# A hybrid RWKV/gMLP block with a mixture of experts: the second norm's shift and the last weight splits on VectorE, the list of further blocks behind the operand transposes, small recurrence matmuls in turn over array parts

## The chip, the cores and the metric

The kernel runs on one core of one Trainium2 chip. The metric is the device time of one execution in microseconds. The numbers below are from repeated timings of the kernel before and from one profiled execution of it. Engines are named as in the profile: PE is TensorE (PEld its weight loads), DVE is VectorE, ACT is ScalarE, POOL is GpSimd, and SP is SyncE, whose queue starts most of the large transfers.

## The reference

One decoder block over a sequence of 1024 tokens of width 1024, all in float32. A first norm with a shift and scale computed from the vector c, one projection for two mixers (causal gMLP on half the width, RWKV-7 recurrence on the other half), one output projection, a second norm with its own shift and scale, and a mixture of 32 experts in 4 groups, two experts to a token. Cut to what the change touches:

```python
def _modulate(h, shift, scale):
    return h * (1 + scale[:, None, :]) + shift[:, None, :]

def reference(x, c, ...):
    mod = c @ ada_w[l] + ada_b[l]
    shift1, scale1, gate1, shift2, scale2, gate2 = jnp.split(mod, 6, axis=-1)
    h = _modulate(_rmsnorm(x, norm1_g[l]), shift1, scale1)
    z = h @ w_in[l]
    y_a = _gmlp_mixer(...)
    y_b = _rwkv7_mixer(...)
    y = jnp.concatenate([y_a, y_b], axis=-1) @ w_out[l]
    x = x + gate1[:, None, :] * y
    h = _modulate(_rmsnorm(x, norm2_g[l]), shift2, scale2)
    y = _hier_moe(h, router_group_w[l], ..., w_gate[l], w_up[l], w_down[l])
    x = x + gate2[:, None, :] * y
    return _rmsnorm(x, final_norm_g)
```

In `_rwkv7_mixer` a state of 64x64 for each of 8 heads runs through all tokens: it decays, is corrected along one vector and takes up the product of key and value; the output is state times r. In `_hier_moe` each token takes the best of 4 groups and in it the best two of 8 experts, and each expert computes `(silu(x @ w_gate) * (x @ w_up)) @ w_down` for its tokens.

## The kernel before

Work runs through four stages. **First** the vector c is turned into shifts, scales and gates, the first norm is taken and its result is split into a high and a low part, because the large products run as sums of products of such parts. Weights that come from HBM are split in the same way by `Stream.split`: ScalarE copies the high part (L282), another engine subtracts it from the raw weight (L284); `stream.eng` names that engine.

**Second** come the projection and the recurrence, for four quarters `q` of the sequence (`rwkv_unit`, L537 on; a quarter is a unit). A unit forms its products between keys and queries chunk by chunk (GR: `pch<-AR,kb`, L552, scaled into `GM`), solves a triangular system by blocks of 16 and 32 (L586 to L645: `pch<-s,GM`, `pch<-GM,s`), and carries the state over four chunks (L647 to L712: `akv` and the solve `pu` write two tiles, the state products `pch<-S,AR` and `py<-S,AR` use the old state S). Its matmuls use parts of the 128x128 array: 16, 32 or 64 rows and as many columns. The projection's large matmuls (`mm<-h,w`, `mm<-w,h`) are handed in between as filler.

**Third** is the output projection with the residual, in halves. Its last part (`outproj_b1`, L979 on) takes the second pair of `w_out` tiles through `Stream.split` with `stream.eng = [nc.gpsimd]` (`w<-wt,w`). Beside it `Rows.norm` normalises two row tiles at a time: VectorE scales (L1093), GpSimd adds the shift with a permuted read, so that a row lies in the order that the experts read (L1094), and the row is stored to `h2d` (L1095). Then follows the routing on VectorE (L1102 to L1185): logits L, group and expert choice by maxima and masks, the mask Mc of chosen experts, running counts, slots, and the table `tabT`. `expert_counts` sorts the experts by count; `tables` makes the index `idx` and weights `wrep` from `tabT`, `limits` the bounds `dg` and the counts `cnt`.

**Fourth** are the experts in sorted order (`positions`). Weight tiles of 2 MB go through a ring of nine; four places are loaded early, five use memory that is only free when the last row has been stored to `h2d`. A `Block` gathers the quarter rows of up to 128 tokens from `h2d` (L1527), transposes them to `xT` (L1534), multiplies them with gate and up weights (`mm<-wt,xT`), applies the activation and multiplies with the down weights (`pch<-wt,aT`). Position n + 1 is transposed and n + 2 gathered while n is computed. `lists` (L1600 to L1666) makes, in steps, the list of further blocks for experts with more tokens than their place holds; a last loop works on that list. At the end the rows are gathered back and the last norm is taken.

All of this is generated as one program, and the order on each engine is set by a scheduler that places instructions by priority as their operands become ready in its own account of time; each engine then runs its instructions strictly in that order. So a change of one instruction can move others that it doesn't name. `tc.issue_after(i)` tells the scheduler not to place what follows ahead of i.

## Time and profile before

| what | us |
|---|---|
| median of 3 runs | 1466.57 (1464.32 to 1468.75) |
| profiled execution | 1464.12 |
| its span in the trace | 1462.4 |
| PE / DVE / POOL / ACT busy | 1244.2 / 622.7 / 518.1 / 334.2 |
| DMA | 336.96 MB, mean 230 GB/s |

The span leaves 1.7 us of the profiled execution around it. Busy shares here are averages over the four stages, which have different limits; the rows below are therefore taken by stretch. In a timeline row the bracket names the idle time of the engine ahead of the instruction and what ended it. A busy vector instruction is not always a working one: an instruction that should be short and is long was held up after its start.

### The profile page before, as it was taken

The numbers are of one execution on the slowest core, as the hardware profiler recorded it, in microseconds if no ns is written. First come the engines' busy times: TensorE is split into PE (matmuls) and PEld (weight loads), VectorE is DVE, ScalarE is ACT, GpSimd is POOL, SyncE is SP. The second block draws the span as 40 slices with busy tenths as digits, with TensorE's granted clock in tenths as the row PEclk, the third lists the DMA queues.
The fourth block names the chain that finished last, engine by engine and source line by source line (L and its number), as shares of the span: only waits on it lengthen the run. The fifth ranks groups of instructions, "written<-read, shape, count | busy, mean of one in ns | idle before, by whom it ended". The sixth has DMA issues, their size and how long they took to land. (4 is left out here: it accounts for less than half of the span.)

```text
span 1462.4 us, 35772 instructions
## 1 busy us (share of the span) xinstructions
PE 1244.2 (85%) x15245; PEld 989.1 (68%) x15245; DVE 622.7 (43%) x1495; ACT 334.2 (23%) x619; POOL 518.1 (35%) x585
## 2 busy tenths in 40 slices
PE   4898888999997899989988449999999999989740
PEld 1576786768885788889975326686877788857520
DVE  2643853683246773772259761122111211112127
ACT  3634442233253543313232100000000000000002
POOL 4555421652354343542375652222111211110015
PEclk9989858997998879899987659999999999999875
DMA  8346325352225312340056388999999999999957
GB/s 309 91 141 235 104 62 159 89 173 74 58 69 174 94 38 66 102 163 31 23 212 252 144 342 290 398 416 410 417 415 413 354 418 417 417 416 382 375 192 282
DMA packets 125330, 336.96 MB, mean 230 GB/s; under 512 B 17016, under 2 KB 77364, under 8 KB 100592
## 3 DMA queue, kind: packets, MB, share of 16 engines
q1 hardware_dynamic: 88784, 273.44, 49.6%
q0 software_dynamic: 13584, 38.06, 7.0%
q10 hardware_dynamic: 22800, 23.12, 4.7%
q8 instruction: 122, 2.00, 0.6%
q14 instruction: 40, 0.33, 0.1%
HBM read 299.54 MB, written 38.44 MB: 231 GB/s over the span
## 5 line engine op out<-in xcount | busy, mean ns | idle before, releaser
L59 PE MATMUL mm<-wt,xT 128*32 128x256 f32 x5760 | 351.0, 385 | 46.4 <-issue 24.5
L59 PEld LDWEIGHTS mm<-wt,xT 128*32 128x32 f32 x5760 | 262.8, 111 | 123.9 <-issue 54.5
L59 PE MATMUL mm<-h,w 128*128 128x512 f32 (+2 forms) x864 | 225.9, 415 | 8.3 <-DVE h L354 3.2
L1527 POOL DMA_INDIRECT xg<-h2d,idx x90 | 92.3, 1026 | 354.2 <-DVE xT L1534 332.0
L59 PEld LDWEIGHTS mm<-h,w 128*128 128x128 f32 (+2 forms) x864 | 162.8, 194 | 55.0 <-DVE h L354 7.3
L59 PE MATMUL pch<-wt,aT 128*32 128x256 f32 x2880 | 184.5, 380 | 5.5 <-DVE yo L1576 1.7
L284 POOL TENSOR_TENSOR w<-wraw,w 128x512 fp32r<-128x512 f32 (+2 forms) x104 | 135.8, 1307 | 146.3 <-ACT w L282 145.3
L59 PEld LDWEIGHTS pch<-wt,aT 128*32 128x32 f32 x2880 | 130.6, 110 | 48.5 <-issue 20.0
L1554 DVE SCALAR_TENSOR_TENSOR sp<-mm,wrep,sg 128x128 f32<-128x128 f32 x90 | 31.9, 424 | 253.4 <-ACT sg L1551 253.4
L59 PE MATMUL mm<-w,h 128*128 128x256 f32 (+1 forms) x816 | 130.1, 313 | 8.3 <-DVE b L895 2.5
L1551 ACT ACTIVATE sg<-mm 128x256 f32<-128x256 f32 (+1 forms) x52 | 17.8, 355 | 488.6 <-PE mm L59 315.0
L59 PEld LDWEIGHTS mm<-w,h 128*128 128x128 f32 x816 | 114.0, 206 | 16.4 <-issue 2.9
L282 ACT ACTIVATE w<-wraw 128x512 fp32r<-128x512 f32 (+2 forms) x104 | 63.6, 614 | 95.4 <-PE mm L59 50.5
L59 PEld LDWEIGHTS pch<-s,GM 16*32 16x32 f32 (+2 forms) x1280 | 62.4, 134 | 18.2 <-DVE s L613 8.0
L59 PE MATMUL pch<-s,GM 16*32 16x16 f32 (+3 forms) x1280 | 66.8, 207 | 8.2 <-DVE s L613 7.0
L1534 DVE STREAM_TRANSPOSE xT<-xg 128x768 f32<-128x768 f32 (+2 forms) x33 | 29.4, 894 | 100.1 <-PE mm L59 100.1
L1576 DVE TENSOR_TENSOR yo<-pch,gate 128x512 f32<-128x512 f32 (+1 forms) x52 | 30.3, 610 | 76.5 <-PE pch L59 45.4
L1747 POOL DMA_INDIRECT wt<-ysd,rowi x16 | 16.6, 1036 | 98.4 <-DMA ysd<-yo 93.8
L59 PE MATMUL py<-aw,ccol 128*1 128x256 f32 x320 | 32.2, 476 | 16.4 <-DMA aw<-in_ada_w_dram 13.8
L556 DVE SCALAR_TENSOR_TENSOR GM<-pch,nsq,gmask 128x128 f32<-128x128 f32 x128 | 35.4, 339 | 2.5 <-PE pch L59 2.1
L59 PE MATMUL pch<-AR,kb 64*128 64x128 f32 x256 | 35.0, 327 | 0.9 <-DVE kb L473 0.9
L59 PEld LDWEIGHTS pch<-AR,kb 64*128 64x128 f32 x256 | 30.8, 225 | 6.0 <-issue 1.6
(418 smaller groups left out, 1645.8 us busy)
## 6 DMA issues: line engine op xcount, KB each, us to landing
wt<-in_moe_w_gate_dram SPq DMA_DIRECT2D x64, 1024.0 KB
wt<-in_moe_w_up_dram SPq DMA_DIRECT2D x64, 1024.0 KB
wt<-in_moe_w_down_dram SPq DMA_DIRECT2D x64, 1024.0 KB
aw<-in_ada_w_dram SPq DMA_DIRECT2D x48, 512.0 KB
wraw<-in_w_in_dram SPq DMA_DIRECT2D x80, 256.0 KB
ysd<-aw POOLq DMA_DIRECT2D x1, 8192.0 KB
ysd<-yo ACTq DMA_DIRECT2D x56, 96.0 KB
wraw<-in_w_out_dram SPq DMA_DIRECT2D x16, 256.0 KB
```

The source lines that it names most:

```text
L59: nc.tensor.matmul(*a_, **k_)
L282: nc.scalar.activation(hi, raw, AF.Copy)
L284: eng.tensor_tensor(lo, raw, hi.bitcast(F32), op=OP.subtract)
L556: nc.vector.scalar_tensor_tensor(GM[:, u, :], pg[:, c * P:(c + 1) * P], nsq[:, u:u + 1], gmask, op0=OP.mult, op1=OP.mult)
L1527: tc.keep_in_program_order(nc.gpsimd.indirect_dma_start(out=self.xg[:, 256 * g:256 * g + 256], out_offset=None, in_=h2q, in_offset=bass.In ...
L1534: nc.vector.transpose(self.xT[:, 0:self.ng].rearrange("p g k t -> p (g k t)"), self.xg[:, 0:256 * self.ng])
L1551: nc.scalar.activation(sg[:, g0:g0 + m, :], v[:, :, 0, :], AF.Silu)
L1554: nc.vector.scalar_tensor_tensor(self.sp[:, g0 + g, :].rearrange("p (b j) -> p j b", b=4), perm(v[:, g, 1, :]), self.wt(g0 + g), perm(sg[: ...
L1576: nc.vector.tensor_tensor(yo[:, g0:g0 + m, :], po[g0 // 2][:, 0:256 * m].rearrange("p (g f) -> p g f", g=m), gate2.unsqueeze(1).to_broadca ...
L1747: nc.gpsimd.indirect_dma_start(out=part(t, j), out_offset=None, in_=ysd, in_offset=bass.IndirectOffsetOnAxis(ap=rowi[:, t, j:j + 1], axis=0))
```

## The change

Five edits. The shift of the second norm is added by VectorE instead of GpSimd. The low parts of the last weights are subtracted by VectorE instead of GpSimd. The tensor `h2d` has 128 further rows, which an early store fills with zeros; the first three blocks' gathers carry no bounds check, the tiles that they fill are taken in another order and only their last quarter is cleared. `limits`, those clears and each step of `lists` are issued behind the latest operand transpose. In the recurrence the products over the two row halves, of the solve's two parts, of `akv` and `pu`, and of the two uses of the old state are written in turn, the last for even chunks only.

```diff
-    h2d = dram.tile([S, D], F32, name="h2d")
+    h2d = dram.tile([S + P, D], F32, name="h2d")
...
+            pgs = [c512() for h in range(2)]
+            for c in range(4):
+                for h in range(2):
+                    r = slice(64 * h, 64 * h + 64)
+                    mm_(pgs[h][:, c * P:(c + 1) * P], kb[r, c, :, :].rearrange("p a t -> p (a t)"),
+                                     AR[l][r, c, :, :].rearrange("p a t -> p (a t)"), start=True, stop=True)
             for h in range(2):
-                r = slice(64 * h, 64 * h + 64)
-                pg = c512()
...
+        pt = c512()
+        for u in range(32):
+            for b, r in enumerate((lo, hi)):
+                r16 = slice(r.start, r.start + 16)
+                mm_(pt[r, u * 16:(u + 1) * 16], GM[r16, u, 32 * b:32 * b + 32], AY[r16, u, 0:16], start=True, stop=True,
+                    skip_group_check=True)
         for b, r in enumerate((lo, hi)):
-            pt = c512()
...
+            if c % 2 == 0:
+                py = psy.tile([P, 512], F32, name="py")
+            t0 = (c % 2) * 64
...
+                    if t0 == 0:
+                        out_state(l)
...
+            pr, one = akv(c + 1) if c < 3 else (None, lambda *hd: None)
             for l, h, r, o in heads:
                 mm_(pu[64:128, o], GM[64:128, l * 8 + 2 * c + h, 0:64], R[64:128, o], start=True, stop=True)
+                one(l, h, r, o)
...
-        stream.eng = [nc.gpsimd]
+        stream.eng = [nc.vector]
...
-                nc.gpsimd.tensor_tensor(h2.rearrange("t (a b j) -> t a b j", a=4, b=KT), perm(tmp), perm(O["sh2"]), op=OP.add)
+                nc.vector.tensor_tensor(h2.rearrange("t (a b j) -> t a b j", a=4, b=KT), perm(tmp), perm(O["sh2"]), op=OP.add)
...
+        nc.gpsimd.dma_start(h2d[S:S + P, :], zt_)
...
-    for t_ in xgs:
-        nc.vector.memset(t_, 0.0)
...
+            skip = dict(bounds_check=4 * S - 1, oob_is_err=False) if Block.turn >= 3 else {}
+            self.xg = xgs[Block.turn % 3]
...
-    O["limits"]()
+    with tc.issue_after(Block.last.ins):
+        for t_ in xgs:
+            nc.vector.memset(t_[:, 768:1024], 0.0)
+        O["limits"]()
...
         if n > 1:
-            next(listing, None)
+            with tc.issue_after(Block.last.ins):
+                next(listing, None)
```

Lines of the changed kernel have other numbers: the scaling of the second norm is L1093 before and L1111 now, the shift addition L1094 and L1112, the mean's reduction L1102 and L1120, `limits` L1045 to L1052 and L1063 to L1070, the transposes L1534 and L1552, the clears L1509 and L1619.

VectorE at the last two row tiles, where `r` is the reciprocal root of the mean square, `b` the rows and L the logits. Before:

```order
L1102 TENSOR_REDUCE r_8000<-ss_7671 128x2 [waits Activation_49]
L145 TENSOR_SCALAR r_8000<-r_8000 128x2 [waits DVE_49]
L1085 TENSOR_TENSOR L<-mm,L 128x72 [waits PE_49]
L1104 TENSOR_TENSOR L<-L,r_8000 128x72 [waits DVE_49,Pool_49]
L1093 SCALAR_TENSOR_TENSOR b_8006<-b_7667,r_8000,b_6928 128x1024
L1105 TENSOR_TENSOR L<-L,RB 128x72 [waits DVE_49]
L1112 TENSOR_REDUCE gm<-L 128x2 [waits DVE_49]
L1113 TENSOR_TENSOR gq<-L,gm 128x8 [waits DVE_49]
L1146 TENSOR_TENSOR ex<-L,gm 128x2x4
```

Now:

```order
L1120 TENSOR_REDUCE r_7993<-ss_7664 128x2 [waits Activation_49]
L145 TENSOR_SCALAR r_7993<-r_7993 128x2 [waits DVE_49]
L1111 SCALAR_TENSOR_TENSOR b_7999<-b_7660,r_7993,b_6921 128x1024 [waits Pool_49]
L1195 TENSOR_TENSOR tabT<-tabT,tt 64x192 [waits PE_49]
L1112 TENSOR_TENSOR b_8000<-b_7999,b_6922 128x1024 [waits DMAHW5_49,DVE_49]
L1111 SCALAR_TENSOR_TENSOR b_8004<-b_7662,r_7993,b_6921 128x1024 [waits DVE_49]
L1103 TENSOR_TENSOR L<-mm,L 128x72 [waits PE_49]
L1112 TENSOR_TENSOR b_8005<-b_8004,b_6922 128x1024 [waits DMASW0_49,DVE_49]
L1122 TENSOR_TENSOR L<-L,r_7993 128x72 [waits DVE_49]
L1123 TENSOR_TENSOR L<-L,RB 128x72 [waits DVE_49]
L1130 TENSOR_REDUCE gm<-L 128x2 [waits DVE_49]
```

Both scalings and both shift additions now stand ahead of the routing's first maximum (`gm`); before, one scaling stood ahead of it, the other some twenty rows behind, and the additions were on GpSimd.

VectorE between the table `tabT` and the first expert, where `idx` is the index of the gathers, `sort` and `dg` belong to `limits`, `xg` is a gathered tile and `l_...` belong to `lists`. Before (the first transpose stands some forty rows of `lists` further on):

```order
L1046 TENSOR_REDUCE sort<-sort 64x1 [waits DVE_49]
L1047 TENSOR_SCALAR dg<-ident,sort 32x32 [waits DVE_49]
L1177 TENSOR_TENSOR tabT<-tabT,tt 64x192 [waits PE_49]
L1509 MEMSET xg_8172 128x1024 [waits DMASW7_49,DMASW6_49,DMAHW0_49,DMASW5_49,DMAHW1_49,DMASW1_49,Pool_49]
L1030 CAST eid<-tt 1x32 [waits PE_49]
L1509 MEMSET xg_8173 128x1024
L1509 MEMSET xg_8174 128x1024
L1630 MEMSET ov 1x99
L1639 MEMSET l_9098 1x32
L1038 TENSOR_SCALAR idx<-tt,acol 128x192 [waits PE_49]
L1052 COPY cnt<-tt 128x96 [waits PE_49]
L1609 TENSOR_TENSOR l_8740<-cnt 128x32 [waits DVE_49]
```

Now:

```order
L1195 TENSOR_TENSOR tabT<-tabT,tt 64x192 [waits PE_49]
L1048 CAST eid<-tt 1x32 [waits PE_49]
L1056 TENSOR_SCALAR idx<-tt,acol 128x192 [waits PE_49]
L1552 STREAM_TRANSPOSE xT<-xg_8165 128x768 [waits DMASW6_49,DMASW7_49,DMASW3_49,DMAHW0_49,DMASW2_49,DMASW0_49]
L1619 MEMSET xg_8165 128x256
L1619 MEMSET xg_8166 128x256
L1619 MEMSET xg_8167 128x256
L1063 TENSOR_TENSOR sort<-sort,posc 64x32 [waits DVE_49]
L1552 STREAM_TRANSPOSE xT<-xg_8166 128x768 [waits DMASW3_49,DMASW2_49,DMASW1_49]
L1064 TENSOR_REDUCE sort<-sort 64x1 [waits DVE_49]
L1065 TENSOR_SCALAR dg<-ident,sort 32x32 [waits DVE_49]
```

The transposes now follow the index at once, the clears stand behind the first transpose, and the rows of `limits` stand around the transpose of the second block. `dg` for the second bound and `cnt` follow within the next four rows.

TensorE at the same place, where `tt<-dg,ones` is the product of `limits` and `mm<-wt,xT` are the first expert's gate and up products. Before:

```order
L59 MATMUL tt<-sort,tabT 32x32 x23
L59 MATMUL py<-sort,tabT 32x32 x24
L59 MATMUL tt<-Mrun,ones 128x32 [waits DVE_49]
L59 MATMUL tt<-dg,ones 128x64
L59 MATMUL mm<-wt,xT 32x256 [waits DMASW5_49,DMASW2_49,DMASW6_49,DMASW1_49,DMASW7_49,DMASW0_49,DMAHW0_49,DVE_49,DMAHW1_49,PE_49,DMAHW7_49,Activation_49,Pool_49]
L59 MATMUL mm<-wt,xT 32x256 x47
```

Now:

```order
L59 MATMUL tt<-sort,tabT 32x32 x23
L59 MATMUL py<-sort,tabT 32x32 x24
L59 MATMUL tt<-Mrun,ones 128x32 [waits DVE_49]
L59 MATMUL mm<-wt,xT 32x256 [waits DMASW6_49,DMASW3_49,DMASW7_49,DMASW2_49,DMAHW0_49,DMASW1_49,DMAHW4_49,DMASW0_49,DMAHW5_49,DVE_49,DMAHW6_49,PE_49,DMAHW7_49,Activation_49,Pool_49]
L59 MATMUL mm<-wt,xT 32x256 x23
L59 MATMUL tt<-dg,ones 128x64 [waits DVE_49]
L59 MATMUL mm<-wt,xT 32x256 x24
```

The product of `limits` has moved from ahead of the first expert to behind its first 24 matmuls.

## Rows read from the trace of the kernel before

**Rows 1.** Table of windows, four stretches: start and end, length, busy us (and instructions) of each engine, the granted share of TensorE's full clock, the mean busy share of the DMA engines, GB/s.
```profile
60.00:745.00 685.00, 634.61 (x6001) 533.21 (x6001) 360.33 (x891) 256.72 (x449) 290.03 (x340) 0.88 0.33 101
...
757.60:819.90 62.30, 48.24 (x176) 35.99 (x177) 54.24 (x156) 16.28 (x32) 39.15 (x23) 0.72 0.65 257
...
850.40:867.00 16.60, 0.00 (x1) 0.03 (x1) 16.32 (x44) 0.00 (x0) 13.24 (x12) 0.50 1.02 414
...
940.00:1320.00 380.00, 365.64 (x6316) 291.21 (x6318) 72.47 (x147) 13.07 (x38) 68.01 (x68) 0.99 1.01 410
```

**Rows 2.** Timeline of all engines while the last two row tiles are normalised and routed: start us, length us, engine, line, operation, tile written and tiles read, shapes, count, and in brackets the idle time ahead of it with what ended it.
```profile
821.81 3.84 POOL L1094 TENSOR_TENSOR b<-b,b 128x1024 f32<-128x1024 f32 x1
...
822.39 0.16 DVE L1102 TENSOR_REDUCE r<-ss 128x2 f32<-128x4 f32 x1 [0.75 <-ACT b L1075]
...
822.58 3.11 DVE L145 TENSOR_SCALAR r<-r 128x2 f32<-128x2 f32 x1
...
825.77 0.71 POOL L146 TENSOR_TENSOR r<-r,nhalf 128x2 f32<-128x2 f32 x1
...
826.67 1.28 DVE L1093 SCALAR_TENSOR_TENSOR b<-b,r,b 128x1024 f32<-128x1024 f32 x1
...
828.12 0.16 DVE L1112 TENSOR_REDUCE gm<-L 128x2 f32<-128x8 f32 x1
...
828.32 3.52 DVE L1113 TENSOR_TENSOR gq<-L,gm 128x8 f32<-128x8 f32 x1
...
836.07 3.77 POOL L1094 TENSOR_TENSOR b<-b,b 128x1024 f32<-128x1024 f32 x1 [3.40 <-DVE aq L1114]
...
836.18 3.68 DVE L1152 SCALAR_TENSOR_TENSOR sg<-ex,sg 128x2 f32<-128x2 f32 x1
...
840.33 0.22 DVE L1135 TENSOR_TENSOR Mc<-Mall 128x64 f32<-128x64 f32 x1
```

**Rows 3.** The same timeline earlier, in the last output projection: one pair of GpSimd and VectorE.
```profile
765.04 3.88 POOL L1094 TENSOR_TENSOR b<-b,b 128x1024 f32<-128x1024 f32 x1 [1.93 <-DVE b L1093]
...
765.16 3.85 DVE L1161 TENSOR_TENSOR val<-Mall,tokf 128x64 f32<-128x64 f32 x1
```

**Rows 4.** Timeline from the table products to the first expert (the last row from the timeline of TensorE alone, which joins its matmuls).
```profile
847.05 0.81 PE L59 MATMUL py<-sort,tabT 32*32 32x32 f32 x43
...
848.76 0.91 DVE L1509 MEMSET xg<- 128x1024 f32 x1 [0.16 <-issue]
...
849.74 0.37 DVE L1038 TENSOR_SCALAR idx<-tt,acol 128x192 int32<-128x192 f32 x1
...
850.40 1.17 POOL L1527 DMA_INDIRECT xg<-h2d,idx  x1 [3.59 <-DVE cnt L1052]
...
854.49 1.00 POOL L1527 DMA_INDIRECT xg<-h2d,idx  x1 [0.30 <-issue]
...
865.72 1.82 DVE L1534 STREAM_TRANSPOSE xT<-xg 128x768 f32<-128x768 f32 x2
...
867.00 5.26 PE L59 MATMUL mm<-wt,xT 128*32 128x256 f32 x53 [17.96 <-issue]
```

**Rows 5.** DMA queues between 850.4 and 862 us: the queue that carries the gathers, its packets, MB, share of 16 engines.
```profile
q0 software_dynamic: 256, 0.44, 10.1%
```

**Rows 6.** Groups of instructions by line and shape over the whole execution, GpSimd and then VectorE: busy us, mean ns of one, idle us ahead of them and what ended it.
```profile
L1094 POOL TENSOR_TENSOR b<-b,b 128x1024 f32<-128x1024 f32 x8 | 31.0, 3874 | 10.4 <-DVE b L1093 4.1 <-DVE aq L1114 3.4 <-issue 1.6
...
L284 POOL TENSOR_TENSOR w<-wt,w 128x512 fp32r<-128x512 f32 x16 | 21.6, 1363 | 13.0 <-ACT w L282 12.9
...
L942 DVE TENSOR_TENSOR b<-b,b 128x512 f32<-128x512 f32 x4 | 2.6, 682 | 0.0
...
L1751 DVE TENSOR_TENSOR wt<-wt 128x1024 f32<-128x1024 f32 x8 | 9.8, 1223 | 15.6 <-DMA wt<-ysd,rowi 15.4
...
L1554 DVE SCALAR_TENSOR_TENSOR sp<-mm,wrep,sg 128x128 f32<-128x128 f32 x90 | 31.9, 424 | 253.4 <-ACT sg L1551 253.4
```

**Rows 7.** Timeline of SP's queue: the first issue of the ring's second part, and the first reissue into the ring.
```profile
843.87 0.80 SPq L1465 DMA_DIRECT2D wt<-in_moe_w_down_dram  x2
...
882.16 0.34 SPq L1458 DMA_DIRECT2D wt<-in_moe_w_gate_dram  x1
```

**Rows 8.** Table of windows, columns as in rows 1, one stretch of 5 us at the start of the experts.
```profile
875.00:880.00 5.00, 2.75 (x18) 0.76 (x21) 0.00 (x0) 0.00 (x0) 2.81 (x3) 0.80 0.27 67
```

**Rows 9.** Groups of VectorE between 757 and 840 us, columns as in rows 6.
```profile
L1161 DVE TENSOR_TENSOR val<-Mall,tokf 128x64 f32<-128x64 f32 x7 | 8.5, 1217 | 0.0
```

**Rows 10.** Groups of TensorE over the whole execution, columns as in rows 6. A float32 matmul leaves two records, so counts are twice the code's.
```profile
L59 PE MATMUL pch<-AR,kb 64*128 64x128 f32 x256 | 35.0, 327 | 0.9 <-DVE kb L473 0.9
...
L59 PE MATMUL pch<-s,GM 16*32 16x16 f32 x512 | 23.0, 197 | 7.0 <-DVE s L613 7.0
...
L59 PE MATMUL pch<-GM,s 32*16 32x16 f32 x512 | 13.6, 178 | 0.0
```

**Rows 11.** Timeline of TensorE: one set of GR products, one set of products over one row half, and the first and the last of a stretch of 22 rows with 32 records in all, in which two products over the two row halves take turns.
```profile
117.70 1.71 PE L59 MATMUL pch<-AR,kb 64*128 64x128 f32 x16 [0.93 <-DVE kb L473]
...
673.75 1.14 PE L59 MATMUL pch<-VU,GM 64*64 64x64 f32 x16
...
678.90 0.50 PE L59 MATMUL pch<-s,GM 64*64 64x64 f32 x5
...
679.99 0.45 PE L59 MATMUL pch<-VU,GM 64*64 64x64 f32 x5
```

More of the change, by code (lines that the diff above doesn't have):

```diff
@@ L626, in rwkv_unit @@
         nc.vector.tensor_tensor(AY[lo, :, 0:16], AY[lo, :, 0:16], pt[lo].rearrange("p (u c) -> p u c", c=16), op=OP.add)
+        pt = c512()
+        for u in range(32):
+            for b, r in enumerate((lo, hi)):
+                r16 = slice(r.start, r.start + 16)
+                mm_(pt[r16, u * 16:(u + 1) * 16], Y[r, u, :], GM[r, u, 32 * b + 16:32 * b + 32], start=True, stop=True,
+                    skip_group_check=True)
         for b, r in enumerate((lo, hi)):
[L628 removed]
             r16 = slice(r.start, r.start + 16)
[L630 to L631 removed]
             nc.scalar.activation(GM[r16, :, 32 * b + 16:32 * b + 32], pt[r16].rearrange("p (u c) -> p u c", c=16), AF.Copy)
@@ L650, in akv, with one @@
             pr = c512()
-            for l, h, r, o in heads:
+            def one(l, h, r, o):
                 mm_(pr[64:128, o], GM[0:64, l * 8 + 2 * c + h, 0:64], VU[0:64, c, o], start=(l + h == 0),
                                  stop=(c + q == 0), skip_group_check=True)
-            return pr
+            return pr, one
         halves = ((slice(0, 256), nc.vector), (slice(256, 512), nc.scalar))
@@ L666, in rwkv_unit @@
         X["buf"] = [ec.tile([P, 33, 32], F32, name=f"s{i}").rearrange("p a b -> p (a b)") for i in range(2)]
-        pr = akv(0)
+        pr, one = akv(0)
+        for hd in heads:
+            one(*hd)
         py = None
```

31 lines of the change are left out of this document (10 added, 21 removed).

## The prediction

> **What bounds the kernel now.** I read the table of windows first, because one share of busy time would average over stages with different limits [rows 1]. Three limits stand in it. From 60 to 745 us (recurrence, with the input projection as filler) TensorE is busy for 634.61 of 685 us: nothing else comes near, so time taken out of its queue there is time saved, as long as the filler is ready. From 940 to 1320 us the DMA engines are busy all the time at 410 GB/s: the experts' weights bound this stage, and it can only begin earlier, not run faster. Between them lie the last output projection (757.6 to 819.9 us) and the routing. In the first VectorE is busy for 54.24 of 62.30 us and TensorE for 48.24; from 850.4 to 867 us TensorE does nothing.
>
> Then I read the timeline of the routing [rows 2]. A vector instruction of 0.15 us lasts 3.1 to 3.7 us wherever GpSimd is in its 3.8 us addition of the second norm's shift: the reduced sum's scaling (L145) at 822.58, L1113 at 828.32, L1152 at 836.18. The earlier rows show the same pair at 765 us [rows 3]. So GpSimd's additions are not beside VectorE's work but in its way.
>
> Last I followed the start of the experts backwards [rows 4]: first gate/up matmul 867.00, its operand's transpose 865.72, first gather 850.40, index 849.74. The index waits behind three clears of 0.91 us, though its matmuls end at 847.86. The transposes come straight behind VectorE's list of further blocks, while 0.44 MB, more than the first block's three gathers of 128 rows of 1 KB (0.39 MB), have landed by 862 us [rows 5].
>
> **The routing and the start of the experts.** I keep 822.39, where the sums of squares of the last rows arrive, as the fixed point. Before, 17.94 us lie between it and Mc at 840.33. In the new order both scaled rows and both shift additions stand ahead of the routing chain, on VectorE. The reciprocal root is ready at 822.39 + 0.16 + 0.16 + 0.71 + 0.1 of gaps = 823.5 [rows 2]. Two scalings of 1.28, two additions of X, and about 1.0 of small ones follow. The chain from the group maximum (828.12) to Mc then takes 12.21 (to 840.33), less the two stalls of 3.37 and 3.54 and less a scaling of 1.28 that stood in it: 4.0 [rows 2].
>
> X is not in the trace: VectorE has no addition that permutes 1024 elements. The contiguous one takes 1.22 [rows 6]; the same permuted addition on GpSimd takes 3.87 [rows 6]. A vector instruction that scatters its output in steps takes 0.42 for 128 elements [rows 6], which by length would be 3.4. I take 2.2, the middle in ratio of 1.22 and 3.87, and keep both as bounds. The Trainium skill ("Advanced Engine Details and Errata", SBUF Cachelines) says that going to another 16-byte line at each access costs extra, and the permuted reads do that in steps of 32 bytes; it gives no price, so by it the sum only lies above that of 1.22.
>
> With 2.2: 823.5 + 2.56 + 4.4 + 1.0 + 4.0 = 835.5 at Mc, 4.8 earlier. Without the clears the index follows its matmuls at once (849.74 against 847.86, 1.9), and the gather no longer waits for the count behind it (0.2): 6.9 in all, first gather at 843.5. The last h2d rows are written some 8 us earlier, and with them the ring's next 10 MB of weights, which SP issues from 843.87 on [rows 7]: the gathers still travel under full queues, so I leave their 11.6 us (850.40 to 862), landing at 855.1. Now the transposes come next on VectorE, 0.91 each [rows 4]; first matmul at 856.3 against 867.00: 10.7 earlier.
>
> One wait is new. TensorE's queue has 24 gate/up matmuls, then tt<-dg,ones, which needs two vector results that stand behind the transpose of the second block. That block's gathers follow 4.1 us behind (854.49 against 850.40) [rows 4], so its transpose can begin at 859.2 and dg is there at about 861. The 24 matmuls are 48 records at 53 in 5.26 us [rows 4]: TensorE comes to the wait at 861.1. I take 1 us, with 3 as upper bound; the rest of block one and everything after is queued behind it. SP reissues weights at 882.16, 15.2 us behind the first matmul [rows 7], and the engines stand at 27% DMA share meanwhile [rows 8]: this moves with TensorE. From there on the stage is DMA bound, so what is won here reaches the end: **10 us** (4 with X of 3.87 and 3 of wait, 13 with X of 1.22 and none). The list of further blocks now runs between the experts, where VectorE is busy for 72 of 380 us [rows 1]; I cost it at nothing. If it did delay an operand's transpose, its steps of up to 1.2 us would show as TensorE waiting. The zero rows are one 0.5 MB store in the first stages, where the DMA share is 0.33 [rows 1]: nothing.
>
> **The last output projection.** 16 splits leave GpSimd (1.36 each) for VectorE, where a subtraction of this length takes 0.68 [rows 6]: 10.9 us, and four of the additions, 8.8 with X of 2.2. Against these 19.7 go 8.1 us of idle VectorE and the stalls. One line alone shows their size: seven L1161 take 8.5 us in all [rows 9], at 0.22 each for Mc of the same size [rows 2], 7.0 lost. Over all small instructions of this stretch I estimate some 20 us. So VectorE ends about where it was, while each split comes 0.7 sooner behind ScalarE. The stretch cannot go below TensorE's 48.24, a gain of 14; if no stall went it would be 12 longer. I take **5 us**.
>
> **The recurrence.** The GR products (pch<-AR,kb) fill 35.0 us of TensorE [rows 10]. With the two row halves in turn, into two tiles, they may overlap. The nearest row: products over one row half take 1.14 for 16, while the same in turn over both halves, as the scheduler already has it for two other products, take 32 in 1.54 (678.90 to 680.44) [rows 11], 48 ns instead of 71, a ratio of 0.68. For GR this gives 11 us; since its records are twice as long, I take 9, between 0 and 17. The first solve stage fills 23.0 us [rows 10], 45 ns a record; its sister with 32 rows has 27 ns (13.6 for 512). Reaching that gives 9; I take 6, between 0 and 9. The Trainium skill ("TensorEngine Tiling (Array Packing)", Gotcha 1: PSUM Pressure) says that row tiles cannot access one PSUM bank at the same time; this stage now writes both row groups into one bank, so by it these 6 are 0 and the sum is 6 less. The remaining solve stage already runs at 27 ns; the new order of the output-state products is hardly realised. Against this: evacuations that ran beside the second half of a stage now begin when both are done, about 1.2 us for each of four units, 5 in all. Net **10 us**, with -8 and +24 as bounds, since the scheduler shuffles the filler anew.
>
> **Sum.** 10 + 5 + 10 = 25 from the profiled execution's 1464.12 gives 1439; the runs' median is 2.45 above that execution, so 1442.
>
> **Rivals.**
> Alternation buys nothing: TensorE takes the two row groups one after the other, and later evacuations eat the rest. For it: GR's 107 ns a record (16 in 1.71 us [rows 11]) may be streaming alone. Against it: the row halves in turn of rows 11. Then the recurrence gives 0, and 15 remain: 1452.
> Alternation pays in full: GR 17 and solve 9, with the filler always ready, less 2: 24 in place of 10, 1428.
> The slower side: VectorE becomes the bound of the output projection. It runs in order, and the splits now stand behind the routing instructions, four scalings and four additions. If the additions take GpSimd's 3.87 there (15.5) and the stalls were not GpSimd's doing, 10.9 + 15.5 - 8.1 = 18 us are added, TensorE waits for each split, and the recurrence gives nothing; the start then gives only 4: 1466.6 + 18 - 4 = 1481. It decides from the point where the added vector time exceeds what the stalls give back by more than the other two gains, 4 to 20 us. Against it: the pairs of rows 2 and 3.
> The start does not come: the gathers land when the weights let them, near 865, whenever they were issued, and the recurrence's gains are taken by the filler's new order. Then only some 3 remain: 1463.
>
> **Chances.** Forecast 0.46, nothing from alternation 0.22, in full 0.13, start does not come 0.10, slower 0.09. About 0.3% (4.4 us) is what a measurement of this kernel can tell from no change. Of these cases the first three are faster (0.81), the fourth is the same (0.10), the last slower (0.09). The range takes in the first three cases, with 8 us below the lowest for bounds that add up, and ends at the fourth, where 2 in 10 are left out: 1420 to 1463; the forecast's own is 1434 to 1450.
>
> **What would show it.** Right: no vector instruction of small size above 0.5 us between 757 and 842; L1112 between 1.2 and 3.9 us; clears behind the transposes; first matmul about 10 us closer to Mc's row; the SP reissue moved alike; pch<-AR,kb clearly below 35.0 us and pch<-s,GM 16*32 below 23.0. Wrong: TensorE waiting for w<-wt of VectorE between the projection's matmuls; a wait for dg of several us; the recurrence ending at the same time as before with less busy time on TensorE.

## The result

The changed kernel takes 1416.84 us (1413.33 to 1419.01, 4 runs) against 1467.38 before (4 runs): a ratio of 0.9656, 95% interval 0.963 to 0.9682. The profiled execution took 1416.36 with a span of 1414.6. It is 50 us faster, where 25 were forecast, and lies below the stated range.

**Where the time came from.** Four marks that both programs have cut the span: the first split of `outproj_b1`, the last rows' mean reduction, the experts' first matmul, and the end. Table of windows between them, before, columns as in rows 1. The first row runs from the first matmul of the first solve stage to the first split, the fourth from the experts' first matmul to the ring's first reissue, the fifth from the start to the reduction:

```profile
188.03:757.58 569.55, 534.62 (x5489) 451.63 (x5489) 294.53 (x730) 200.58 (x358) 233.03 (x257) 0.87 0.31 94
757.58:822.39 64.81, 50.09 (x190) 37.42 (x190) 56.01 (x157) 18.14 (x38) 41.40 (x27) 0.73 0.65 254
822.39:867.00 44.61, 9.37 (x134) 7.22 (x133) 41.31 (x113) 1.00 (x3) 27.15 (x21) 0.51 0.66 261
867.00:882.16 15.16, 11.81 (x103) 4.99 (x107) 0.54 (x1) 0.00 (x0) 9.99 (x10) 0.75 0.57 208
0.00:822.39 822.39, 727.46 (x6475) 595.29 (x6475) 450.76 (x1144) 304.94 (x548) 369.12 (x447) 0.87 0.39 125
```

The same stretches of the changed kernel:

```profile
181.53:724.72 543.19, 509.76 (x5487) 426.75 (x5486) 299.07 (x728) 203.28 (x365) 228.71 (x261) 0.88 0.32 97
724.72:778.55 53.83, 42.41 (x196) 34.35 (x197) 51.17 (x180) 20.05 (x42) 5.16 (x6) 0.82 0.85 347
778.55:809.60 31.05, 12.45 (x149) 9.53 (x148) 16.90 (x63) 1.74 (x4) 10.63 (x14) 0.55 0.73 289
809.60:834.82 25.22, 14.14 (x107) 7.05 (x111) 2.58 (x10) 0.00 (x0) 13.66 (x14) 0.59 0.59 220
0.00:778.55 778.55, 689.93 (x6457) 561.85 (x6458) 449.38 (x1165) 303.93 (x546) 324.90 (x427) 0.89 0.41 133
```

Up to the first split 757.58 became 724.72, 32.9 us won (forecast 10). The recurrence's own last product (`py<-VU,GM`) ends at 723.0 before and at 687.2 now, so the mark stands for the recurrence. The output projection went from 64.81 to 53.83, 11.0 won (forecast 5). From the reduction to the first matmul 44.61 became 31.05, 13.6 won. And from there to the end 595.4 became 605.0: 9.6 were given back, all of them before the first reissue, since from the reissue on it takes 580.2 and 579.8. 32.9 + 11.0 + 13.6 - 9.6 = 47.9, against 47.8 of the spans.

The marks do not divide the work sharply: in some of the kernels below, work that here comes ahead of the last reduction comes behind it, so that one stretch is shorter by some 10 us and the next longer. Where this happens, I give the sum from the first split to Mc, which is 82.75 before and 66.54 here.

**The ring.** The experts' stage is bound by its transfers (rows 1), so it can also be read from SP's queue. Timeline of the changed kernel, answering to rows 7:

```profile
790.62 0.80 SPq L1484 DMA_DIRECT2D wt<-in_moe_w_down_dram  x2
...
834.82 0.35 SPq L1477 DMA_DIRECT2D wt<-in_moe_w_gate_dram  x1
```

The ring's second part is issued 53.3 us earlier than before (843.87), and from that issue to the end it takes 624.0 us in place of 618.5. Between that issue and the first reissue the DMA engines are busy for a share of 0.75 of 44.2 us, before for 0.81 of 38.3: they stand idle for 11.0 us in place of 7.3.

**The recurrence.** Groups of TensorE over the whole execution, answering to rows 10:

```profile
L59 PE MATMUL pch<-AR,kb 64*128 64x128 f32 x256 | 28.8, 328 | 4.5 <-DVE GM L558 3.6 <-DVE kb L473 0.9
...
L59 PE MATMUL pch<-s,GM 16*32 16x16 f32 x512 | 10.9, 186 | 1.8 <-DVE s L615 1.7 <-DVE s L616 0.2
...
L59 PE MATMUL pch<-GM,s 32*16 32x16 f32 x512 | 8.0, 176 | 1.1 <-issue 1.1
```

The first solve stage fell from 23.0 to 10.9 us, 21 ns a record; its sister from 13.6 to 8.0, 16 ns; GR from 35.0 to 28.8. That is 23.9 us less. TensorE's busy time up to the first split fell by 29.9 in all (677.4 to 647.5) and its idle time by 3.0 (80.2 to 77.2), which makes up the 32.9.

**The routing.** Timeline of the last two row tiles and of the index, answering to rows 2 and 4:

```profile
778.55 0.16 DVE L1120 TENSOR_REDUCE r<-ss 128x2 f32<-128x4 f32 x1 [0.73 <-ACT b L1093]
...
778.74 0.17 DVE L145 TENSOR_SCALAR r<-r 128x2 f32<-128x2 f32 x1
...
781.27 2.03 DVE L1112 TENSOR_TENSOR b<-b,b 128x1024 f32<-128x1024 f32 x1
...
784.68 1.98 DVE L1112 TENSOR_TENSOR b<-b,b 128x1024 f32<-128x1024 f32 x1
...
790.89 0.16 DVE L1170 SCALAR_TENSOR_TENSOR sg<-ex,sg 128x2 f32<-128x2 f32 x1
...
791.26 0.22 DVE L1153 TENSOR_TENSOR Mc<-Mall 128x64 f32<-128x64 f32 x1
...
798.33 0.42 DVE L1056 TENSOR_SCALAR idx<-tt,acol 128x192 int32<-128x192 f32 x1 [0.89 <-PE tt L59]
...
799.04 1.10 POOL L1545 DMA_INDIRECT xg<-h2d,idx  x1 [1.18 <-DVE idx L1056]
```

The scaling L145 and L1170 (L1152 before) are back at 0.16 and 0.17 us, from 3.11 and 3.68. The permuted addition takes 2.0 on VectorE. From the reduction to Mc it is 12.7, from Mc to the first gather 7.8, against 17.9 and 10.1. From Mc to the end it is 623.3, against 622.1: behind Mc nothing is won.

**The start of the experts.** Timeline of TensorE from its first expert matmul:

```profile
809.60 4.53 PE L59 MATMUL mm<-wt,xT 128*32 128x256 f32 x42 [10.20 <-issue]
...
814.76 0.38 PE L59 MATMUL mm<-wt,xT 128*32 128x256 f32 x1 [0.63 <-issue]
...
816.90 0.59 PE L59 MATMUL mm<-wt,xT 128*32 128x256 f32 x1 [1.76 <-issue]
...
825.37 0.58 PE L59 MATMUL mm<-wt,xT 128*32 128x256 f32 x1 [2.23 <-issue]
...
827.98 0.47 PE L59 MATMUL tt<-dg,ones 32*128 32x64 f32 x1
...
829.10 10.87 PE L59 MATMUL mm<-wt,xT 128*32 128x256 f32 x144
```

After 42 records the matmuls come one by one, 2.8 us apart, with "issue" as the reason: nothing that the trace shows is waited for. The two small products of `limits` stand in the middle of this and not behind a wait: their vector results were there at 814.2. Only at 829.1 does TensorE run again. GpSimd's timeline in the same time, the first and the last of its gathers:

```profile
799.04 1.10 POOL L1545 DMA_INDIRECT xg<-h2d,idx  x1 [1.18 <-DVE idx L1056]
...
823.61 1.00 POOL L1545 DMA_INDIRECT xg<-h2d,idx  x1 [0.30 <-issue]
```

Between them GpSimd issues gather after gather, and two scatters (L1207), with pauses of 0.3 us; two more scatters follow at 825.77 and 829.02. Before, there was the same: 53 records, then three to five in 1.4 us up to 878.44, while the gathers ran until 878.4. One row of TensorE's timeline before:

```profile
875.58 0.64 PE L59 MATMUL mm<-wt,xT 128*32 128x256 f32 x5 [0.78 <-issue]
```

I call this the slow stretch. Of the two queues that load instructions, q8 moves nothing and q14 one packet of 0.01 MB between 813 and 829.1 us in the changed kernel, so a late load on q8 does not explain it.

### The profile page after: what moved, and what is told of

It reads as the page before. It is cut to its first block, busy times and chain, and to the rows that moved or that the text cites. A ratio compares the mean times of both kernels' runs of the same rounds, so it can differ in the third digit from the quotient of the medians.

```text
span 1414.6 us, 35774 instructions
## 1 busy us (share of the span) xinstructions
PE 1211.0 (86%) x15245; PEld 960.1 (68%) x15245; DVE 612.7 (43%) x1519; ACT 334.1 (24%) x619; POOL 462.8 (33%) x562
## 5 line engine op out<-in xcount | busy, mean ns | idle before, releaser
L284 POOL TENSOR_TENSOR w<-wraw,w 128x512 fp32r<-128x512 f32 (+2 forms) x104 | 131.6, 1269 | 148.0 <-ACT w L282 147.7
L1569 ACT ACTIVATE sg<-mm 128x256 f32<-128x256 f32 (+1 forms) x52 | 17.9, 355 | 485.8 <-PE mm L59 286.4
L1552 DVE STREAM_TRANSPOSE xT<-xg 128x768 f32<-128x768 f32 (+2 forms) x33 | 29.6, 896 | 113.8 <-PE mm L59 102.1
L59 PE MATMUL pch<-s,GM 16*32 16x16 f32 (+3 forms) x1280 | 54.5, 202 | 5.9 <-DVE s L671 2.7
L59 PEld LDWEIGHTS pch<-s,GM 16*32 16x32 f32 (+2 forms) x1280 | 49.5, 126 | 13.8 <-issue 7.0
L1770 POOL DMA_INDIRECT wt<-ysd,rowi x16 | 17.1, 1068 | 99.2 <-DMA ysd<-yo 94.7
L59 PE MATMUL py<-aw,ccol 128*1 128x256 f32 x320 | 29.6, 453 | 12.1 <-DMA aw<-in_ada_w_dram 11.9
L59 PE MATMUL pch<-AR,kb 64*128 64x128 f32 x256 | 28.8, 328 | 4.5 <-DVE GM L558 3.6
L59 PEld LDWEIGHTS pch<-AR,kb 64*128 64x128 f32 x256 | 24.2, 224 | 10.9 <-DVE GM L558 4.5
```

Of the source, the lines that this page charges most:

```text
L59: nc.tensor.matmul(*a_, **k_)
L284: eng.tensor_tensor(lo, raw, hi.bitcast(F32), op=OP.subtract)
L1552: Block.last = nc.vector.transpose(self.xT[:, 0:self.ng].rearrange("p g k t -> p (g k t)"), self.xg[:, 0:256 * self.ng])
L1569: nc.scalar.activation(sg[:, g0:g0 + m, :], v[:, :, 0, :], AF.Silu)
L1770: nc.gpsimd.indirect_dma_start(out=part(t, j), out_offset=None, in_=ysd, in_offset=bass.IndirectOffsetOnAxis(ap=rowi[:, t, j:j + 1], axis=0))
```

## The experiments

Ratios are to the kernel before on the same chip. Markers are read from each kernel's profile as above. The last six kernels ran on a chip on which the kernel before takes 1454 us, 10 to 15 less than on the others.

### Parts alone

The two solve stages alone:

```diff
+        pt = c512()
+        for u in range(32):
+            for b, r in enumerate((lo, hi)):
...
+                mm_(pt[r, u * 16:(u + 1) * 16], ...)
```

> The kernel before with one part of the change: the two parts of the solve's first and last stage in turn. Theory A (the array's row groups really work at once, and TensorE's queue is what bounds the recurrence): pch<-s,GM 16*32 falls from 23.0 to about 11 us and pch<-GM,s 32*16 from 13.6 to about 8, and the time falls by about the 18 us of both, to about 1449. Theory B (the 33 us won ahead of the projection come from a new order of the filler, whatever part is changed): the two groups shorten, but the time falls by less than 8 or by more than 25 us, without relation to them. By the rule that row tiles cannot use one PSUM bank at once the first group would stay at 23; the trace of the changed kernel already speaks against that.

Measured 0.9982 (0.9954 to 1.0011): 3 us, and within its interval of nothing. Groups and window up to the last reduction:

```profile
L59 PE MATMUL pch<-s,GM 16*32 16x16 f32 x512 | 12.4, 193 | 5.6 <-DVE s L613 3.9 <-DVE s L614 1.7
...
L59 PE MATMUL pch<-GM,s 32*16 32x16 f32 x512 | 7.7, 177 | 0.6 <-issue 0.6
```

```profile
0.00:822.23 822.23, 709.25 (x6472) 575.17 (x6472) 455.89 (x1144) 303.67 (x547) 371.18 (x447) 0.88 0.39 125
```

The groups did what theory A says, and TensorE's busy time fell by 18.2 (727.46 to 709.25). The time did not: idle time rose from 94.9 to 113.0. The waits of TensorE in that kernel (engine, what for; total us, times, longest) show where:

```profile
PE py L59 <- DMA aw<-in_ada_w_dram: 12.9, 7, 2.5
...
PE mm L59 <- DVE b L900: 6.2, 1, 6.2
...
PE mm L59 <- ACT v L1257: 3.1, 2, 2.7
```

Before, the first was 6.9 and the second 2.5. The filler was not there when the shorter stage wanted it. So a smaller time in TensorE's queue is worth something only together with what follows.

GR alone (hunk as in the diff above).

> The kernel before with one part of the change: the GR products over the two row halves in turn, into two PSUM tiles. Theory A: pch<-AR,kb falls from 35.0 to about 29 us, and the time by 4 to 8 us, to about 1461. Theory B (order of the filler): a change of the time by more than 12 us either way.

0.9928 (0.9906 to 0.9951), 10.5 us. GR fell to 25.6, 9.4 less, the 9 of the forecast; busy time up to the reduction 716.51, 10.9 less, idle time 99.3. Here the busy time passed on, and more of it than the 4 to 8 of theory A.

The norm alone: L1094 and the splits on VectorE.

> The kernel before with the second norm's shift and the last splits on VectorE, nothing else. Theory A: nothing before the projection changes (first w<-wt copy within 5 us of 757.6); the stretch from there to the last rows' reduction shrinks from 64.8 by about 11 us, and the routing from that reduction to Mc from 17.9 to about 13; the start of the experts gets some 4 to 5 us of that; the end 10 to 16 us earlier, about 1454. Theory B: the recurrence also ends more than 8 us earlier, since the scheduler orders everything anew.

0.9875 (0.9809 to 0.9941), 18 us. The recurrence ended 9 us later (first split 766.63), which neither theory has. The projection shrank by 20, from 64.8 to 45.0, and the reduction to Mc stayed at 17.1; from the first split to Mc it is 62.08 in place of 82.75. Its two halves, on another chip:

```diff
-                nc.gpsimd.tensor_tensor(h2.rearrange(...), perm(tmp), perm(O["sh2"]), op=OP.add)
+                nc.vector.tensor_tensor(h2.rearrange(...), perm(tmp), perm(O["sh2"]), op=OP.add)
```

> The kernel before with the second norm's shift addition on VectorE, the splits still on GpSimd. Theory A (the additions of 3.9 us hold VectorE and, on GpSimd's queue, the splits behind them): most of the 20 us in the projection and the whole of the gain from the last reduction to Mc; about 1450. Theory B (the splits are the cause): under 6 us in all, about 1461.

```diff
-        stream.eng = [nc.gpsimd]
+        stream.eng = [nc.vector]
```

> The kernel before with the last splits on VectorE, the shift still on GpSimd. Theory A: the splits now wait in VectorE's order behind instructions that GpSimd's additions hold up, so little or nothing is won, 1461 to 1468. Theory B (the splits are the cause): most of the 20 us, about 1450.

Shift: 0.9902 (0.9879 to 0.9925), 14 us; projection 57.6, reduction to Mc 12.6. Splits: 0.996 (0.9939 to 0.998), 6 us; projection 53.2, reduction to Mc 18.9. Neither theory holds alone: of the stretch from the first split to Mc 12.6 go with the shift (70.12) and 10.7 with the splits (72.07), where both together gave 20.7. The kernel before was not profiled on this chip, so its stretches are from another. The splits alone lose part of it again: from Mc to the first matmul it is 30.6 in place of 26.7. One split in the second kernel took 3.26 us, the others 0.68; that an addition on GpSimd held it is argued.

The start of the experts alone (zero rows, no bounds check, clears, limits and list behind the transposes).

> The kernel before with the zero rows, the gathers without bounds check, and clears, limits and the list's steps behind the transposes, nothing else. The first matmul of the experts should come about 8 to 9 us earlier relative to Mc. Theory A (TensorE's first matmuls then crawl for want of instructions while the ring's transfers run, as the changed kernel shows, and the first reissue of a ring tile, 38.3 us behind the ring's start before, comes hardly earlier): the end is 0 to 4 us earlier, about 1465. Theory B (the start passes on to the end): 8 us earlier, about 1458.

0.9957 (0.9932 to 0.9981), 6 us. From Mc to the first matmul 19.4 in place of 26.7, and from there to the reissue 22.1 in place of 15.2: theory A for the stage. The 6 us come mostly from ahead of it: the reduction stood at 815.6 (822.39 before), though no instruction of the recurrence was changed; from Mc to the end it is 619.2 in place of 622.1. So a new order of the filler alone can do as much; the kernels below show still more.

### Parts taken back from the changed kernel

> The changed kernel with the solve's two stages put back to one part after the other. Alone this edit took 16.5 us out of TensorE's busy time and only 3 out of the kernel's, because TensorE waited 11 us more ahead of the projection. Theory A (the edit is worth its busy time wherever the filler is ready, as it is in the changed kernel): about 14 to 18 us slower than the changed kernel, 1431 to 1435. Theory B (parts add up as they do alone): 3 us slower, 1420.

0.9784 (0.9743 to 0.9825) against 0.9656: 18.8 us slower, just above the 14 to 18 of theory A. Groups, and the window up to the reduction:

```profile
L59 PE MATMUL pch<-s,GM 16*32 16x16 f32 x512 | 20.5, 190 | 1.6 <-DVE s L615 1.6
...
L59 PE MATMUL pch<-GM,s 32*16 32x16 f32 x512 | 14.1, 181 | 0.0
```

```profile
0.00:795.76 795.76, 711.01 (x6457) 582.57 (x6458) 447.72 (x1165) 305.19 (x547) 327.60 (x427) 0.87 0.40 131
```

The two groups take 15.7 more than in the changed kernel, and the first split comes 16.4 later (741.13). Up to the reduction busy time rises by 21.1 against the changed kernel's 689.93, the stretch by 17.2. In this company the edit's busy time passes on; alone it was worth 3.

> The changed kernel with the GR products put back to one row half after the other. Alone this edit took 9.4 us of TensorE's busy time and 10.5 of the kernel's; in the changed kernel pch<-AR,kb is only 6.2 below before, with 3.6 of new idle time ahead of it (waiting for the scaling into GM). Theory A (busy time and its waits): 3 to 7 us slower than the changed kernel, about 1422. Theory B (parts add up as alone): 10 slower, 1427. More than 12 or faster: the order of the filler decides.

0.9653 (0.9607 to 0.97): nothing lost, which neither theory has. pch<-AR,kb is 37.5, 8.7 more than in the changed kernel, but the reduction comes at 783.1, busy time 693.58, only 3.7 more: other groups became cheaper in that order.

> The changed kernel with the shift and the last splits back on GpSimd. Theory A (the 18 us that this edit is worth alone lie behind the recurrence and are independent of it): the stretch from the first split to the last reduction goes from 53.8 back to about 65, that from there to Mc from 12.7 to about 18; 12 to 18 us slower, about 1432. Theory B (with the recurrence shorter, another wait takes its place): under 8 us slower.

0.9735 (0.9688 to 0.9783): 11.6 us slower, a little under the 12 to 18 of theory A. Projection 66.2, reduction to Mc 18.3, both as it says; the recurrence unchanged (first split 725.2).

> The changed kernel with clears, limits, bounds checks and the list's steps as before. Theory A (of the 8 us by which the first matmul comes earlier, TensorE's crawl behind it gives nearly all back): Mc to first matmul goes from 18.3 to about 26.7, first matmul to the first reissue from 25.2 to about 15, time 0 to 3 us slower. Theory B (the 6 us that the edit is worth alone): about 1423, with the difference ahead of the projection and not in the start of the experts.

0.9633 (0.9581 to 0.9686): not slower. Mc to the first matmul went back to 26.0, first matmul to reissue to 16.3, so in the stage nothing was lost by taking the edit out: from Mc to the end it is 622.5, in the changed kernel 623.3. Ahead of it the order happened to be better (first split at 718.8, Mc at 783.4 in place of 791.3).

> The changed kernel with akv, pu and the two products with the old state written one after the other again. The scheduler had put akv and pu in turn already, and their groups are unchanged (21.3 against 21.0, 20.5 against 20.4, 18.5 against 18.0, 16.8 twice). Theory A: nothing is lost, within 5 us of the changed kernel by the filler's order. Theory B (this is where the rest of the recurrence's 33 us comes from): 6 to 12 us slower.

0.9719 (0.9688 to 0.9751): 9 us slower, the time of theory B. Window up to the first split:

```profile
0.00:737.79 737.79, 654.80 (x6285) 535.09 (x6285) 411.48 (x995) 288.61 (x515) 322.69 (x422) 0.89 0.38 119
```

The recurrence's end came 13.1 us later than in the changed kernel, with 7.3 more busy and 5.8 more idle time. Then the projection took 44.4 and the reduction to Mc 23.6, in place of 53.8 and 12.7: from the first split to Mc 67.92, 1.4 more. So the loss lies ahead of the first split. The edit's four groups take 21.1, 21.3, 19.0 and 17.5 us, 1.8 more than in the changed kernel (21.3, 20.5, 18.5 and 16.8). This run does not show whether the rest is the edit's or that of a new order of the filler: the kernel of the next section loses as much without a longer solve group.

### One bank or two

```diff
-        pt = c512()
+        pts = [c512() for _ in range(2)]
...
-                mm_(pt[r, u * 16:(u + 1) * 16], ...
+                mm_(pts[b][r, u * 16:(u + 1) * 16], ...
```

> The changed kernel with the two parts of each solve stage in PSUM tiles of their own instead of one. Theory A (row groups that write other partitions of one bank do not disturb each other): pch<-s,GM 16*32 stays at 21 ns a record (10.9 us) and pch<-GM,s 32*16 at 16 (8.0), time within 6 us of the changed kernel, by the filler's order alone. Theory B (the shared bank costs something): both groups shorten by over a fifth.

```profile
L59 PE MATMUL pch<-s,GM 16*32 16x16 f32 x512 | 10.4, 180 | 2.3 <-DVE s L615 1.2 <-DVE s L616 1.1
...
L59 PE MATMUL pch<-GM,s 32*16 32x16 f32 x512 | 8.2, 175 | 3.8 <-issue 3.8
```

The groups stay (10.4 and 8.2 against 10.9 and 8.0): with or without a shared bank the two row groups take the same time. The Trainium skill ("TensorEngine Tiling (Array Packing)", Gotcha 1: PSUM Pressure) says that row tiles cannot access one PSUM bank at the same time. I had read a cost into that, by which the first group would have stayed at 23 us; the trace shows none for these two row groups, which write different partitions of the bank. The time, 0.9726 (0.9694 to 0.9758), is 10 us above the changed kernel, where theory A allowed 6; the first split comes 17.0 later (741.7). Busy time is lower (684.76 up to the reduction) and idle time higher (102.7 against 88.6). The groups answer the question; that the filler was less ready, as in the solve alone, is argued.

### What TensorE's slow stretch hangs on

In all the kernels up to here the time from the first gather to the first reissue was 31 to 36 us, whatever the first matmul did. To see whether the gathers cause that, those from the third position on were held back until the first activation:

```diff
+        if n == 0:
+            nc.gpsimd.tensor_copy(idx2[:, 0, 0:1], positions[0].blocks[0].sg[:, 0, 0:1])
+            nc.gpsimd.tensor_copy(idx2, idx)
```

> The changed kernel, but from the third position on the gathers read a copy of the index that GpSimd makes behind ScalarE's first activation, so that only the first six gathers run while TensorE does its first products. In every trace so far TensorE's slow stretch (one to five records in 1.4 to 2.8 us, nothing waited for) ends 1 to 3 us behind GpSimd's unbroken row of gathers, whether the weights' transfers were then running or not. Theory A (the row of gathers starves TensorE of instructions): no slow stretch; first matmul to first reissue 15 us in place of 25; up to 10 us faster than the changed kernel, about 1407, less what comes back when the held gathers run. Theory B (the ring's 10 MB of weights starve it): the slow stretch stays until the transfers are done, reissue 36 to 44 us behind the ring's start, time within 3 us of the changed kernel.

> The same hold on the kernel without the edits at the start of the experts (clears, limits and list ahead of the transposes). There the slow stretch lay where the DMA engines were busy for only 0.2 to 0.5. Theory A: no slow stretch, first matmul to first reissue falls from 16.3 to about 11, up to 5 us faster than without the hold (1410.8). Theory B: unchanged.

0.9774 (0.9747 to 0.98) and 0.9788 (0.9762 to 0.9814), 17 and 23 us slower than the kernels without the hold. TensorE in the first, GpSimd's held row, and the window of 840 to 850 us:

```profile
812.17 5.35 PE L59 MATMUL mm<-wt,xT 128*32 128x256 f32 x48 [10.35 <-issue]
...
818.01 7.98 PE L59 MATMUL mm<-wt,xT 128*32 128x256 f32 x144
...
835.43 0.64 PE L59 MATMUL mm<-wt,xT 128*32 128x256 f32 x4 [0.80 <-issue]
...
846.75 1.72 PE L59 MATMUL mm<-wt,xT 128*32 128x256 f32 x3 [0.75 <-issue]
...
848.85 9.75 PE L59 MATMUL mm<-wt,xT 128*32 128x256 f32 x89 [0.38 <-issue]
```

```profile
828.34 0.97 POOL L1545 DMA_INDIRECT xg<-h2d,idx  x1 [0.27 <-POOL idx L1727]
...
849.22 1.00 POOL L1545 DMA_INDIRECT xg<-h2d,idx  x1 [0.30 <-issue]
```

```profile
840.00:850.00 10.00, 6.33 (x17) 1.33 (x14) 0.00 (x0) 0.00 (x0) 7.82 (x8) 0.67 0.28 67
```

The first block now runs without a break (first reissue 8.7 us behind the first matmul, 7.7 in the second kernel), and the slow stretch stands under the held row, in the second block, from 835 to 849 (from 839 to 855 in the second kernel). The DMA engines are at 0.28 there, so the weights' transfers are not what TensorE lacks. The place is that of theory A; its times were missed, since the stretch has only moved and got longer.

Then the gathers came in threes, each behind the activation two positions earlier:

```diff
+        if n < PACED:
+            nc.gpsimd.tensor_copy(idx2[:, 0, n + 2:n + 3], positions[n].blocks[0].sg[:, 0, 0:1])
+            nc.gpsimd.tensor_copy(idx2[:, :, n + 2], idx[:, :, n + 2])
```

> The changed kernel; the gathers of positions 2 to 9 each read a copy of their part of the index that GpSimd makes behind ScalarE's activation two positions earlier, so that gathers come in threes with gaps. Theory A (the unbroken row starves TensorE; TensorE has a few us of instructions in hand, and three gathers take 4): no crawl anywhere, first matmul to first reissue about 9 us, and as the DMA engines stood still for some 11 us in the changed kernel, about 10 us faster, 1406. Theory B (the held gathers come too late for their position, or the crawl only moves): not faster than the changed kernel.

> The same pacing on the kernel without the edits at the start of the experts (1410.8). Theory A: first matmul to first reissue from 16.3 to about 9, some 7 us faster, 1403. Theory B: not faster.

0.9642 (0.9612 to 0.9673) and 0.9637 (0.9614 to 0.966). No slow stretch in either, 7.7 and 7.6 us from first matmul to reissue. But the kernels with the unbroken row on the same chip (shift_only and splits_only) had none either, 6.9 and 7.8, so there it did not occur, and the two paced kernels test nothing of theory A. The changed kernel was therefore run beside the paced one:

> The changed kernel as it is, beside the paced one. If this chip shows the crawl (first matmul to first reissue over 15 us): time as measured first, 0.966 of before. If not: reissue 8 us behind the first matmul, and the whole of the earlier start passes on to the end; before is then near 1454 and this kernel near 1454 - 54 = 1400, 0.963.

> The paced kernel, beside the changed one. If this chip shows the crawl in the changed kernel, theory A (the row of gathers is its cause): no crawl here and 8 to 14 us faster than the changed kernel. If the changed kernel shows none: the same time within 4 us. Theory B (the crawl depends on the chip alone): both kernels crawl or neither does, and the times are the same.

It was the same chip again. TensorE in the changed kernel there:

```profile
815.94 5.32 PE L59 MATMUL mm<-wt,xT 128*32 128x256 f32 x48 [10.66 <-DVE xg L1619]
...
821.55 7.98 PE L59 MATMUL mm<-wt,xT 128*32 128x256 f32 x144
```

And SP's queue:

```profile
797.02 0.80 SPq L1484 DMA_DIRECT2D wt<-in_moe_w_down_dram  x2
...
824.41 0.35 SPq L1477 DMA_DIRECT2D wt<-in_moe_w_gate_dram  x1
```

No slow stretch, first gather to reissue 19.1 in place of 35.8, and 1402.08 us, 0.9636 (0.9609 to 0.9663). The DMA engines are busy for 0.98 of the 27.4 us between the two issues, and from the first of them to the end it takes 608.0 in place of 624.0. The paced kernel took 1398.6, 0.9614 (0.9587 to 0.9641): no difference that the intervals allow to claim.

## Why the prediction was wrong

**The recurrence's term, 10 us, failed.** 32.9 us came. In "The first solve stage fills 23.0 us [rows 10], 45 ns a record; its sister with 32 rows has 27 ns" I took the sister's 27 ns for the best that the array gives, put the most for this stage at 9 and took 6; then I wrote "The remaining solve stage already runs at 27 ns" and gave it nothing, though the diff puts that stage in turn too. Measured they are 21 and 16 ns: 12.1 and 5.6 us in place of 6 and 0. GR was sized right (9 forecast; 9.4 alone, 6.2 in the changed kernel). The 5 us that I took off for later evacuations did not come: up to the first split idle time is 77.2, before 80.2. So of the 32.9 the three groups give 23.9, other busy time 6.0 and idle time 3.0; the last two were not forecast, and no run ties them to an edit. Taking the solve back lengthens its groups by 15.7 and moves the first split by 16.4, so it is the largest part that the runs show. What is not shown is why the same edit alone brings 3: its idle time is seen (waits for the adaLN weights' transfers and for the filler's operands), its cause in the scheduler's order is argued.

**The output projection's term, 5 us, was too small.** 11.0 came, 11.6 by taking the edit back (with the routing's part), 20 where it stood alone. The mechanism was right: before, 17 small instructions of VectorE lasted 0.6 to 3.9 us in this stretch; now no small one from the first split to Mc lasts above 0.5. The 16 splits take 0.68 each on VectorE, groups of the changed kernel:

```profile
L1112 DVE TENSOR_TENSOR b<-b,b 128x1024 f32<-128x1024 f32 x8 | 16.3, 2042 | 0.0
...
L284 DVE TENSOR_TENSOR w<-wt,w 128x512 fp32r<-128x512 f32 x16 | 10.9, 684 | 2.0 <-ACT w L282 2.0
```

I had set the added 19.7 us against stalls of some 20 and 8.1 of idle time, and called VectorE about even. The additions in the stretch are six, not four, 12.3 us, so 23.3 were added with the splits; the 17 long instructions, 27.1 before, would take about 3.4 at their lengths of now, 23.7 less. That part of the balance held. What came on top is VectorE's idle time, 8.8 before and 2.7 now, and that its busy time, overlaps counted once, fell by 4.8. I had also left out that the granted clock of the stretch, a mean of 1.2 and 2.4 GHz, is 0.82 in place of 0.73 of the full one; TensorE's own work there takes 42.41 us in place of 50.09. That a split no longer stands on GpSimd's queue behind an addition of 3.9 may have helped; no run separates it.

**The start's step "this moves with TensorE" failed, on the chips with the slow stretch.** The sizes ahead of it were right: X 2.0 (2.2 taken), Mc 12.7 behind the reduction (13.1), gather 2.3 sooner behind Mc (2.1), first matmul 13.6 sooner (10.7), no wait for `dg`. But the reissue followed the first gather and not the first matmul: 35.8 us behind it in the changed kernel, 31.8 before. I had read the slow stretch of before in rows 8 only as ring waiting for TensorE, not asked why TensorE was busy for only 2.75 of 5 us with nothing to wait for, and so gave the earlier start in full: 10 forecast, 4.0 measured (13.6 less 9.6). All of it is the routing's 5.2; behind Mc the stage takes 1.2 longer. On the chip without the slow stretch it is 8.5 from matmul to reissue, but that the earlier start passes on to the end there is not established. From Mc to the end the paced kernel takes 602.3 and the paced kernel without the start's edits 610.8, which would be the whole of it; the changed kernel takes 607.3 there, and shift_only, also without these edits, 606.5.

**Rivals.** "Alternation pays in full" at 1428 was nearest, and still too slow, since its 9 for the solve was the same wrong bound. Its condition, the filler always ready, was not met in the solve alone. "VectorE becomes the bound" was excluded by the projection's window, where VectorE is busy for 51.17 of 53.83 us and the stretch is nevertheless shorter: VectorE is now at its limit there. "The start does not come" holds for the stage in part, as just told.

**What stays open.** Why TensorE is slowed under the row of gathers on some chips and not on one; two kernels on one chip show that the stretch moves with the row, not by what path the row would slow TensorE. And the effect of the filler's order: edits that touch no instruction of the recurrence moved its end by -7 (start alone) to +9 us (norm alone), and against the changed kernel two banks moved it by +17.0 with groups of the same length. So some part of the 32.9 can be a lucky order. Solve, GR, norm and start alone add up to 38 us of the 50.

## What to carry to other kernels

Small matmuls on disjoint row groups, written in turn, are worth measuring themselves: a neighbour's time per record is no bound for them, and a shared PSUM bank did not cost anything here. When a stage starts earlier, look at what follows the start as well: if the same stretch takes longer by what was won, another thing sets its end. Here the slow stretch went with GpSimd's row of gathers, and a stage bound by transfers is better timed from the issue of its transfers and the idle time of the DMA engines than from the first matmul. In a kernel whose order a scheduler sets, judge an edit both alone and by taking it back, since one of the two may show nothing, and hold the difference against what a mere reordering does (10 us here).

## What the runs showed of the hardware

TensorE was slowed to mostly one to five matmul records in 0.7 to 2.8 us while GpSimd issued indirect gathers with pauses of 0.3 us, with the DMA engines at 0.2 to 0.3 as well as at 1.0; moving the gathers moved the slow stretch (835 to 849 us in the held kernel), and one of the chips did not show it at all. Two row groups of 16 rows in turn took 21 ns a record where one group alone took 45, in one PSUM bank or two. A permuted addition of 1024 elements with reads 32 bytes apart took 2.0 us on VectorE and 3.9 on GpSimd; VectorE took 1.22 without the permutation. The Trainium skill ("Advanced Engine Details and Errata", SBUF Cachelines) has a penalty for reads that go to another line each time. The trace agrees in the direction: the permuted addition took 0.8 us longer; that the lines are the reason was not tested.
